# Neighbourhood attention: values and weights each split into two fp32r halves, products of 128 stationary columns, in place of fp32 products

## Chip, cores and metric

The kernel runs on one core of one Trainium2 chip. The metric is device time in microseconds (us) of one execution; lower is better.

## What is computed

One layer of an encoder trunk, on two requests with the same weights: a prompt of 512 tokens ("sequence 0") and a sample of 1024 tokens ("sequence 1"). In the layer a projection feeds two attention branches, a global one (GQA) and a neighbourhood one; their outputs are merged by gates, and a dense MLP follows. The change touches the neighbourhood branch only. Cut to that branch (8 heads of 64 channels, tokens on a grid 64 wide, each token attending to a window of 8 rows by 16 columns):

```python
s = jnp.einsum('bqhd,bqwhd->bhqw', qi, kg).astype(jnp.float32) * scale + bi[None]
p = jax.nn.softmax(s, axis=-1).astype(v.dtype)
return jnp.einsum('bhqw,bqwhd->bqhd', p, vg)
```

All inputs and outputs are fp32.

## The kernel before

The kernel is written with a framework that lists instructions in program order, orders them on each engine by priority and readiness, and places the waits. Nearly all DMAs are issued from one queue, that of SyncE (SP). Nearly every product of the kernel is done in fp32r, a one-pass fp32 format of the TensorE, with each operand split into a high half (a ScalarE copy rounds it to fp32r) and a low half (VectorE subtracts the high half from the original): `wunit` (L93, L94) does that for weights, `mm3` (L112 to L114) multiplies high by high, high by low and low by high.

`run` weaves generators: while an attention (`gqa`, then `na`) of one sequence runs, the projections or gates of another are woven in between, so that TensorE has other work ("fill"). In `attention(0)`, the attention of the prompt, the fill is the projection `proj` of the two halves of the sample (its last step writes the values `vb` to DRAM, L483 to L490). In `attention(1)` the fill is `gates` of the sample and then `out_merge` of the prompt.

`na` works through items (head h, row tile rt, column block b): 8 heads times 4 items in sequence 0, with 256 keys each (`ng` = 2 groups of 128), and 8 heads times 8 items in sequence 1, with 384 keys each (`ng` = 3). For an item:

- `softmax` (L651): two score matmuls S (L658, fp32r, queries stationary); VectorE adds the bias and takes the maximum (L661, L662); ScalarE takes the exponential (L665); VectorE inverts the sum and scales (L666, L667).
- `values` (L670): `ng` transposes on TensorE into the PSUM tile T (L674), then one ScalarE copy T to `pt` (L676).
- `weigh` (L679): `ng` products in plain fp32 (L681), with 64 columns of V stationary and 128 columns of `pt` moving, accumulated into the PSUM tile A. It is issued one item later than `values`.
- `finish` (L684), after four items: VectorE copies A to `o` (L686), and SP stores `o`.

Between heads, `load(h)` brings V, Q and K. V is loaded for two heads at once (16 DMAs, L620, only when h is even), in front of Q (L623) and four K loads (L108) on the SP queue; it has two buffers, one for each pair of heads. `load(h+1)` and the bias table of head h+2 (L636) are issued with the first item of head h.

Of the kernel before, what the change touches and what calls it, by code (L numbers as in the profile page):

```python
# [10 lines left out]
F32 = mybir.dt.float32  # L11
F32R = mybir.dt.float32r
BF16 = mybir.dt.bfloat16
AF = mybir.ActivationFunctionType
ALU = mybir.AluOpType
AX = mybir.AxisListType

P = 128
D = 1024
KT = D // P  # L20
CH = 512
TT = CH // P
GW = 64
HD = 64
# [3 lines left out]
KC0 = (0, 8, 24, 32)  # L28
# [11 lines left out]
class Kern:  # L40
# [371 lines left out]
    def proj(self, ch, U, pool):  # L412
        nc, a = self.nc, self.a
        seq, t0 = ch
        sl = slice(t0, t0 + CH)
        s = self.scr[seq]
        ws = self.stream([a["wq"][i] for i in range(4)] + [a["wkv"][i] for i in range(2)]
                         + [a["wst"][i] for i in range(8)] + [a["wvb"][i] for i in range(4)])
        tq, tk = self.rope_tables(pool, t0)
        done = 0  # L420
        ps = []
        for _ in self.tokmajor(U, ws, 2, 512, ps):
            done += 1
            yield done / 18.0
        rq = []
        for t in range(TT):
            r = pool.tile([P, 512], F32, tag="rq", name="rq", bufs=4)
            nc.scalar.activation(r, ps[t], AF.Copy)
            rq.append(r)
        rk = []  # L430
        norm = self.rope_norm(pool, rq, rk)
        next(norm)
        ps = []
        for _ in self.tokmajor(U, ws, 4, 256, ps):
            done += 1
            yield done / 18.0
        for t in range(TT):
            r = pool.tile([P, P], F32, tag="rk", name="rk", bufs=4)
            nc.scalar.activation(r, ps[t][:, 0:128], AF.Copy)
            rk.append(r)  # L440
            vh = pool.tile([P, 2, 2, HD], F32R, tag="vhl", name="vhl", bufs=2)
            pv = ps[t][:, 128:256].rearrange("p (k d) -> p k d", d=HD)
            nc.scalar.activation(vh[:, :, 0, :], pv, AF.Copy)
            nc.vector.tensor_tensor(vh[:, :, 1, :], pv, vh[:, :, 0, :], op=ALU.subtract)
            r = t0 + t * P
            nc.sync.dma_start(s["va"][r:r + P, :], vh.bitcast(F32).rearrange("p a b d -> p (a b d)"))
        next(norm)
        q2, k2 = [], []

        def q_rope(t):  # L450
            q2.append(self.rope(pool, rq[t], 8, rs[0][:, t * 8:t * 8 + 8], tq[:, 0, t], tq[:, 1, t]))

        def k_rope(t):
            k2.append(self.rope(pool, rk[t], 2, rs[1][:, t * 2:t * 2 + 2], tk[:, 0, t], tk[:, 1, t]))

        def q_stack(hp):
            self.pair_stack(pool, q2, hp, [s["qa"][2 * hp + j][:, sl] for j in range(2)])

        def k_stack(_):
            self.pair_stack(pool, k2, 0, [s["ka"][j][:, sl] for j in range(2)])  # L460

        todo = {2: [(q_rope, 0)], 3: [(q_rope, 1), (k_rope, 0)], 4: [(q_rope, 2), (k_rope, 1)],
                5: [(q_rope, 3), (k_rope, 2)], 6: [(k_rope, 3)],
                7: [(q_stack, 0)], 8: [(q_stack, 1)], 9: [(q_stack, 2)], 10: [(q_stack, 3)], 11: [(k_stack, 0)]}
        for i in range(8):
            ps = self.wstat(next(ws), [U])[0]
            if i < 4:
                self.stack(pool, ps, [s["qb"][2 * i + j][:, sl] for j in range(2)], perm=True)
            else:
                self.stack(pool, ps, [s["kb"][2 * (i - 4) + j][:, sl] for j in range(2)], scale=0.125)  # L470
            if i == 2:
                rs = next(norm)
            for f, x in todo.get(i, ()):
                f(x)
            done += 1
            yield done / 18.0
        ps = []
        for j, _ in enumerate(self.tokmajor(U, ws, 2, 512, ps)):
            for f, x in todo.get(8 + j, ()):
                f(x)  # L480
            done += 1
            yield done / 18.0
        for t in range(TT):  # L483
            v = pool.tile([P, CH], F32, tag="vb", name="vb", bufs=2)
            nc.scalar.activation(v, ps[t], AF.Copy)
            r = t0 // GW + 2 * t
            for hp in range(4):
                for i in range(2):
                    c0 = (r % 4 + i) * GW
                    nc.sync.dma_start(s["vb"][hp][c0:c0 + GW, r // 4], v[i * GW:(i + 1) * GW, hp * P:(hp + 1) * P])  # L490

    def gates(self, chs, Us, pool, func):
        nc, a = self.nc, self.a
# [104 lines left out]
    def na(self, seq, pool, psp):  # L598
        nc, a = self.nc, self.a
# [10 lines left out]
        def load(h):  # L610
            if h in heads:
                return heads[h]
            if h % 2 == 0:
                V = pool.tile([P, 4, rows // 4, P], F32, tag="V", name="V", bufs=2)
                src = s["vb"][h // 2]
                for i in range(4):
                    vr = V[i * 32:(i + 1) * 32]
                    for b in range(4):
                        c0 = i * GW + KC0[b]
                        nc.sync.dma_start(vr[:, b], src[c0:c0 + 32])  # L620
                vals[h // 2] = V
            Q = pool.tile([P, T], F32R, tag="Q", name="Q", bufs=2)
            nc.sync.dma_start(Q.bitcast(F32), s["qb"][h])  # L623
            K = []
# [43 lines left out]
            return p  # L668

        def values(h, rt, b, p, acc):  # L670
            V = vals[h // 2]
            tp = psp.tile([P, NK], F32, tag="T", name="T", bufs=2 if nrt > 1 else 1)
            for g in range(ng):
                nc.tensor.transpose(tp[:, g * P:(g + 1) * P], p[:, g * P:(g + 1) * P], self.ident)  # L674
            pt = pool.tile([P, NK], F32, tag="pt", name="pt", bufs=2)
            nc.scalar.activation(pt, tp, AF.Copy)  # L676
            return lambda: weigh(h, rt, b, V, pt, acc)

        def weigh(h, rt, b, V, pt, acc):  # L679
            for g in range(ng):  # L680
                nc.tensor.matmul(acc[0:64, b * P:(b + 1) * P], V[:, b, rt + g, (h % 2) * 64:(h % 2) * 64 + 64],  # L681
                                 pt[:, g * P:(g + 1) * P], start=g == 0, stop=g == ng - 1)

        def finish(h, rt, acc):  # L684
            o = pool.tile([64, CH], F32, tag="o", name="o", bufs=2)
            nc.vector.tensor_copy(o.rearrange("p (r b c) -> p b r c", b=4, c=16),  # L686
                                  acc[0:64].rearrange("p (b r c) -> p b r c", b=4, c=16))
            nc.sync.dma_start(s["ob"][h * 64:(h + 1) * 64, rt * CH:(rt + 1) * CH], o)

        items = [(h, rt, b) for h in range(8) for rt in range(nrt) for b in range(4)]  # L690
# [235 lines left out]
    def scratch(self):  # L926
        self.scr = []
        for q in range(2):
# [2 lines left out]
            self.scr.append(dict(  # L931
                qa=[t(f"qa{h}_", [P, T]) for h in range(8)], ka=[t(f"ka{h}_", [P, T]) for h in range(2)],
                va=t("va_", [T, 2 * P]), qb=[t(f"qb{h}_", [P, T]) for h in range(8)],
                kb=[t(f"kb{h}_", [P, T]) for h in range(8)], vb=[t(f"vb{h}_", [256, T // 256, P]) for h in range(4)],
                g=[t(f"g{i}_", [P, T]) for i in range(16)], oa=t("oa_", [512, T]), ob=t("ob_", [512, T]),
                x1=t("x1_", [T, D]), u2=[t(f"u2{i}_", [P, T]) for i in range(KT)]))

# [251 lines left out]
```

## Time and profile before

| | |
|---|---|
| median of 3 runs | 2530.9 us (2529.63 to 2534.13) |
| profiled execution, its own time | 2528.55 us |
| its span in the trace | 2526.8 us |
| mean granted TensorE clock | 0.975 of full speed |
| TensorE busy | 2388.2 us (95%) |
| TensorE weight loads | 1898.6 us (75%) |
| VectorE busy | 1472.3 us (58%) |
| ScalarE busy | 971.3 us (38%) |
| GpSimd busy | 330.1 us (13%) |
| DMA, mean | 129 GB/s |

Busy time of TensorE is the sum of matmuls whose ends are modelled; neighbouring matmuls overlap, so their spacing (the difference of two starts) is what one costs, and it is shorter than the duration of one. PE is TensorE's matmul side, PEld its weight loads (the stationary operand), DVE is VectorE, ACT ScalarE, POOL GpSimd, SPq the SyncE queue that issues DMAs. The neighbourhood items of sequence 0 lie at about 490 to 637 us of the span, those of sequence 1 at about 950 to 1157 us.

### The profile page before, as it was taken

The page shows a single profiled execution, that of the slowest core. Times are in us where ns is not written, and L with a number is a line of the kernel's source. Part 1 is how long each engine was busy: PE and PEld are TensorE (multiplying, and loading weights), DVE is VectorE, ACT ScalarE, POOL GpSimd, SP SyncE. Part 2 cuts the span into 40 slices and gives each one's busy share as a digit, 9 for nine tenths or more (in the row PEclk, how much of TensorE's full clock was granted, in tenths as well). Part 3 has the DMA queues.
Part 4 walks back from the last instruction along what each step waited for, and adds up shares of the span by engine and source line. Part 5 has one row for each costly group of instructions (what it writes and reads, how often), then busy time and mean ns, then how long its engine had stood idle before and what let it go on. Part 6 is the DMA issues. An engine that isn't in the chain of part 4 may idle for free.

```text
span 2526.8 us, 29800 instructions
## 1 busy us (share of the span) xinstructions
PE 2388.2 (95%) x10992; PEld 1898.6 (75%) x10992; DVE 1472.3 (58%) x2511; ACT 971.3 (38%) x1589; POOL 330.1 (13%) x278
## 2 busy tenths in 40 slices
PE   5987899979999999989998999999999999999997
PEld 4876777756777777767776788887788888888876
DVE  7987677565477763575867754445733333333466
ACT  4434456434577763554334223222412211221222
POOL 4210021230000003331202000003100000000133
PEclk9998899989999999999999999999999999999999
DMA  6757744565512117585656525334511210211231
GB/s 248 245 185 238 213 119 145 141 187 174 157 55 66 58 50 184 148 235 189 202 188 206 191 69 159 99 90 126 176 40 45 61 48 26 67 50 34 68 116 59
DMA packets 134851, 325.86 MB, mean 129 GB/s; under 512 B 21392, under 2 KB 34224, under 8 KB 134704
## 3 DMA queue, kind: packets, MB, share of 16 engines
q1 hardware_dynamic: 134128, 322.86, 41.8%
q0 software_dynamic: 288, 1.05, 0.3%
q8 instruction: 87, 1.43, 0.2%
q14 instruction: 60, 0.49, 0.1%
q10 hardware_dynamic: 288, 0.03, 0.0%
HBM read 261.99 MB, written 62.93 MB: 129 GB/s over the span
## 4 chain that ended last, share of the span: by engine, by line
PE 68%; DVE 12%; DMA 8%; issue 4%; ACT 3%; POOL 2%; SPq 1%; POOLq 0%; ACTq 0%; DVEq 0%
PE D L112 18%; PE D L114 18%; PE D L113 18%; PE S L535 3%; PE T L553 3%; DVE wlo L94 2%; PE A L681 2%; PE A L566 2%; PE A L567 1%; DMA wraw<-in_wada 1%; PE T L674 1%; DVE junk L248 1%; DMA wraw<-in_wst 1%; ACT whi L93 1%; PE S L658 1%
## 5 line engine op out<-in xcount | busy, mean ns | idle before, releaser
L93 ACT ACTIVATE whi<-wraw 128x1024 fp32r<-128x1024 f32 x266 | 279.4, 1057 | 828.2 <-PE D L114 396.9
L114 PE MATMUL D<-uh,wlo 128*128 128x512 f32 x1344 | 537.2, 400 | 20.5 <-DVE wlo L94 20.5
L112 PE MATMUL D<-uh,whi 128*128 128x512 f32 x1344 | 538.3, 400 | 14.1 <-ACT whi L93 12.5
L113 PE MATMUL D<-ul,whi 128*128 128x512 f32 x1344 | 533.9, 397 | 0.0
L94 DVE TENSOR_TENSOR wlo<-wraw,whi 128x1024 fp32r<-128x1024 f32 x266 | 334.8, 1261 | 336.5 <-ACT whi L93 325.8
L114 PEld LDWEIGHTS D<-uh,wlo 128*128 128x128 f32 x1344 | 256.5, 191 | 78.9 <-DVE wlo L94 23.0
L112 PE MATMUL D<-whi,hh 128*128 128x512 f32 x768 | 304.8, 398 | 6.3 <-ACT hh L864 6.3
L112 PEld LDWEIGHTS D<-uh,whi 128*128 128x128 f32 x1344 | 257.3, 191 | 70.1 <-ACT whi L93 13.8
L114 PE MATMUL D<-whi,hl 128*128 128x512 f32 x768 | 303.7, 397 | 0.8 <-DVE hl L865 0.6
L113 PE MATMUL D<-wlo,hh 128*128 128x512 f32 x768 | 303.4, 397 | 0.0
L113 PEld LDWEIGHTS D<-ul,whi 128*128 128x128 f32 x1344 | 257.0, 191 | 54.7 <-issue 0.5
L886 DVE TENSOR_TENSOR y<-y,D 128x512 f32<-128x512 f32 x168 | 115.1, 685 | 214.8 <-PE D L114 214.2
L112 PEld LDWEIGHTS D<-whi,hh 128*128 128x128 f32 x768 | 145.4, 189 | 43.8 <-ACT hh L864 10.2
L114 PEld LDWEIGHTS D<-whi,hl 128*128 128x128 f32 x768 | 145.3, 190 | 37.3 <-DVE hl L865 3.7
L113 PEld LDWEIGHTS D<-wlo,hh 128*128 128x128 f32 x768 | 145.5, 189 | 33.6
L847 POOL TENSOR_TENSOR y<-y,g 128x1024 f32<-128x1024 f32 x12 | 28.8, 2402 | 867.4 <-DVE y L886 867.4
L538 DVE TENSOR_REDUCE m<-S 128x1 f32<-128x1024 f32 (+1 forms) x96 | 99.7, 1041 | 51.7 <-PE S L535 51.2
L557 DVE TENSOR_TENSOR pl<-T,ph 128x512 fp32r<-128x512 f32 x160 | 107.4, 684 | 16.4 <-ACT ph L556 15.0
L556 ACT ACTIVATE ph<-T 128x512 fp32r<-128x512 f32 x160 | 93.4, 597 | 55.5 <-PE T L553 53.1
L112 PE MATMUL D<-whi,uh 128*128 128x512 f32 (+1 forms) x288 | 105.5, 371 | 2.8 <-ACT whi L93 2.2
L647 POOL TENSOR_TENSOR wm<-Wb,mask 128x384 f32<-128x384 f32 (+1 forms) x96 | 78.4, 830 | 198.4 <-DVE m L661 118.8
L113 PE MATMUL D<-wlo,uh 128*128 128x512 f32 (+1 forms) x288 | 103.6, 360 | 0.0
(159 smaller groups left out, 3700.1 us busy)
## 6 DMA issues: line engine op xcount, KB each, us to landing
wraw<-in_w SPq DMA_DIRECT2D x132, 512.0 KB, 3.7
wraw<-in_wst SPq DMA_DIRECT2D x56, 512.0 KB, 5.4
wraw<-in_wada SPq DMA_DIRECT2D x32, 512.0 KB, 4.3
g<-gst SPq DMA_DIRECT2D x48, 256.0 KB, 2.3
og<-g SPq DMA_DIRECT2D x48, 256.0 KB, 3.2
wraw<-in_wab SPq DMA_DIRECT2D x24, 512.0 KB, 5.2
wraw<-in_wo SPq DMA_DIRECT2D x24, 512.0 KB, 5.1
raw<-in_wada_k SPq DMA_DIRECT2D x16, 512.0 KB, 8.2
```

The source lines that it names most:

```text
L93: nc.scalar.activation(hi, raw, AF.Copy)
L94: (engine or nc.vector).tensor_tensor(lo, raw, hi, op=ALU.subtract)
L112: mm(out, l[0], r[0], start=start, stop=False)
L113: mm(out, l[0], r[1], start=False, stop=False)
L114: mm(out, l[1], r[0], start=False, stop=stop)
L535: nc.tensor.matmul(S[:, k * CH:(k + 1) * CH], q, K[r][:, k * CH:(k + 1) * CH], start=r == 0, stop=r == 1)
L538: nc.vector.tensor_reduce(m, S[:, :T], axis=AX.X, op=ALU.max, negate=True)
L553: nc.tensor.transpose(tp[:, qt * P:(qt + 1) * P], Ps[qt][:, k * P:(k + 1) * P], self.ident)
L556: nc.scalar.activation(ph, tp, AF.Copy)
L557: nc.vector.tensor_tensor(pl, tp, ph, op=ALU.subtract)
L647: nc.gpsimd.tensor_tensor(wm.rearrange("p (r c) -> p r c", c=32), wv, mask[:, rt * 4 + b, :].rearrange("p (r c) -> p r c", c=32), op=ALU.add)
L886: nc.vector.tensor_tensor(y[:, hs], y[:, hs], ps, op=ALU.add)
```

## The change

The values are written to DRAM with the high and the low fp32r half of each head side by side (64 columns each), four heads to a scratch tensor. V is loaded for each head instead of for each pair of heads; a head's V now holds 128 columns (high, low), so a V tile is as large as before. The transposed weights are split too: ScalarE writes the high half `ph`, VectorE the low half `pl`. `weigh` runs 2 times `ng` fp32r products with 128 stationary columns (high and low of V) in place of `ng` fp32 products with 64. The upper 64 partitions of A then hold the low half's part, and `finish` adds them (one ScalarE copy more).

```diff
         for t in range(TT):
-            v = pool.tile([P, CH], F32, tag="vb", name="vb", bufs=2)
-            nc.scalar.activation(v, ps[t], AF.Copy)
             r = t0 // GW + 2 * t
-            for hp in range(4):
+            for hf in range(2):
+                v = pool.tile([P, 4, 2, HD], F32R, tag="vb", name="vb", bufs=2)
+                pv = ps[t][:, hf * 256:(hf + 1) * 256].rearrange("p (h d) -> p h d", d=HD)
+                nc.scalar.activation(v[:, :, 0, :], pv, AF.Copy)
+                nc.vector.tensor_tensor(v[:, :, 1, :], pv, v[:, :, 0, :], op=ALU.subtract)
+                vf = v.bitcast(F32).rearrange("p a b d -> p (a b d)")
                 for i in range(2):
                     c0 = (r % 4 + i) * GW
-                    nc.sync.dma_start(s["vb"][hp][c0:c0 + GW, r // 4], v[i * GW:(i + 1) * GW, hp * P:(hp + 1) * P])
+                    nc.sync.dma_start(s["vb"][hf][c0:c0 + GW, r // 4], vf[i * GW:(i + 1) * GW])
...
-            if h % 2 == 0:
-                V = pool.tile([P, 4, rows // 4, P], F32, tag="V", name="V", bufs=2)
-                src = s["vb"][h // 2]
-                for i in range(4):
-                    vr = V[i * 32:(i + 1) * 32]
-                    for b in range(4):
-                        c0 = i * GW + KC0[b]
-                        nc.sync.dma_start(vr[:, b], src[c0:c0 + 32])
-                vals[h // 2] = V
+            V = pool.tile([P, 4, rows // 4, P], F32R, tag="V", name="V", bufs=2)
+            src = s["vb"][h // 4][:, :, h % 4 * P:(h % 4 + 1) * P]
+            for i in range(4):
+                vr = V[i * 32:(i + 1) * 32].bitcast(F32)
+                for b in range(4):
+                    c0 = i * GW + KC0[b]
+                    nc.sync.dma_start(vr[:, b], src[c0:c0 + 32])
+            vals[h] = V
...
-            pt = pool.tile([P, NK], F32, tag="pt", name="pt", bufs=2)
-            nc.scalar.activation(pt, tp, AF.Copy)
-            return lambda: weigh(h, rt, b, V, pt, acc)
-
-        def weigh(h, rt, b, V, pt, acc):
-            for g in range(ng):
-                nc.tensor.matmul(acc[0:64, b * P:(b + 1) * P], V[:, b, rt + g, (h % 2) * 64:(h % 2) * 64 + 64],
-                                 pt[:, g * P:(g + 1) * P], start=g == 0, stop=g == ng - 1)
+            ph = pool.tile([P, NK], F32R, tag="pt", name="ph", bufs=2)
+            pl = pool.tile([P, NK], F32R, tag="pl", name="pl", bufs=2)
+            nc.scalar.activation(ph, tp, AF.Copy)
+            nc.vector.tensor_tensor(pl, tp, ph, op=ALU.subtract)
+            return lambda: weigh(b, rt, V, (ph, pl), acc)
+
+        def weigh(b, rt, V, pt, acc):
+            for j in range(2):
+                for g in range(ng):
+                    nc.tensor.matmul(acc[:, b * P:(b + 1) * P], V[:, b, rt + g, :], pt[j][:, g * P:(g + 1) * P],
+                                     start=j == 0 and g == 0, stop=j == 1 and g == ng - 1)
 
         def finish(h, rt, acc):
-            o = pool.tile([64, CH], F32, tag="o", name="o", bufs=2)
-            nc.vector.tensor_copy(o.rearrange("p (r b c) -> p b r c", b=4, c=16),
-                                  acc[0:64].rearrange("p (b r c) -> p b r c", b=4, c=16))
+            lo = pool.tile([64, CH], F32, tag="ot", name="ot", bufs=1)
+            nc.scalar.activation(lo, acc[64:128], AF.Copy)
+            o = pool.tile([64, CH], F32, tag="o", name="o", bufs=2 if nrt > 1 else 1)
+            nc.vector.tensor_tensor(o.rearrange("p (r b c) -> p b r c", b=4, c=16),
+                                    acc[0:64].rearrange("p (b r c) -> p b r c", b=4, c=16),
+                                    lo.rearrange("p (b r c) -> p b r c", b=4, c=16), op=ALU.add)
...
-                kb=[t(f"kb{h}_", [P, T]) for h in range(8)], vb=[t(f"vb{h}_", [256, T // 256, P]) for h in range(4)],
+                kb=[t(f"kb{h}_", [P, T]) for h in range(8)], vb=[t(f"vb{h}_", [256, T // 256, CH]) for h in range(2)],
```

## Rows read from the trace of the kernel before

**Rows 1.** Stretches: length; busy PE, PEld, DVE, ACT, POOL; granted clock, DMA share, GB/s.
```profile
490.00:628.00 138.00, 115.50 (x530) 83.95 (x528) 81.68 (x238) 55.96 (x137) 32.82 (x44) 0.89 0.61 179
950.00:1157.00 207.00, 196.83 (x1058) 147.84 (x1057) 116.10 (x373) 94.87 (x226) 68.80 (x70) 0.98 0.67 178
```

**Rows 2.** Timeline of PE, a burst of items in sequence 1: start, us, group.
```profile
1057.73 0.62 PE L658 MATMUL S<-K,Q 128*128 128x384 f32 x2
1058.27 0.87 PE L681 MATMUL A<-pt,V 128*64 128x128 f32 x6
1059.07 0.55 PE L674 MATMUL T<-ident,P 128*128 128x128 f32 x3
1059.38 0.96 PE L658 MATMUL S<-K,Q 128*128 128x384 f32 x4
1060.18 0.49 PE L674 MATMUL T<-ident,P 128*128 128x128 f32 x3
1060.60 0.87 PE L681 MATMUL A<-pt,V 128*64 128x128 f32 x6
```

**Rows 3.** Timeline of PE, one item in sequence 0.
```profile
525.95 0.65 PE L681 MATMUL A<-pt,V 128*64 128x128 f32 x4
526.53 0.50 PE L112 MATMUL D<-uh,whi 128*128 128x512 f32 x1
```

**Rows 4.** Timeline of PE, then of PEld: fp32r, 128 stationary columns, 256 moving.
```profile
318.30 0.28 PE L114 MATMUL D<-whi,ul 128*128 128x256 f32 x1
318.42 0.28 PE L112 MATMUL D<-whi,uh 128*128 128x256 f32 x1
...
318.30 0.19 PEld L112 LDWEIGHTS D<-whi,uh 128*128 128x128 f32 x1
```

**Rows 5.** The bounds: PE, 512 moving columns; PEld, loads before transposes.
```profile
1049.75 0.39 PE L112 MATMUL D<-uh,whi 128*128 128x512 f32 x1
1049.98 0.40 PE L113 MATMUL D<-ul,whi 128*128 128x512 f32 x1
...
1059.07 0.31 PEld L674 LDWEIGHTS T<-ident,P 128*128 128x128 f32 x3 [0.17 <-issue]
```

**Rows 6.** Groups by line and shape: busy, mean ns, idle before it.
```profile
L681 PE MATMUL A<-pt,V 128*64 128x128 f32 x512 | 81.6, 293 | 5.0 <-ACT pt L676 4.8
L674 PEld LDWEIGHTS T<-ident,P 128*128 128x128 f32 x256 | 30.1, 146 | 27.7 <-issue 12.1 <-ACT pt L676 4.5 <-PE T L674 2.0
L557 DVE TENSOR_TENSOR pl<-T,ph 128x512 fp32r<-128x512 f32 x160 | 107.4, 684 | 16.4 <-ACT ph L556 15.0
L661 DVE CUSTOM_DVE_ANT_0 sb<-S,wm 128x384 f32<-128x384 f32 x64 | 34.9, 550 | 53.6 <-PE S L658 51.7 <-PE T L674 1.3 <-POOL wm L647 0.3
L667 DVE TENSOR_SCALAR P<-P,z 128x384 f32<-128x384 f32 x64 | 31.0, 485 | 1.2
L575 DVE TENSOR_TENSOR o<-A,ot 64x512 f32<-64x512 f32 x24 | 16.3, 681 | 3.2 <-ACT ot L573 2.7
L686 DVE COPY o<-A 64x512 f32<-64x512 f32 x24 | 16.3, 678 | 5.8 <-PE A L681 5.7
L573 ACT ACTIVATE ot<-A 64x512 f32<-64x512 f32 x24 | 14.3, 596 | 9.1 <-PE A L567 8.8
```

**Rows 7.** Timeline of the SP queue: V and K loads, and value stores.
```profile
493.51 14.39 SPq L620 DMA_DIRECT2D V<-vb  x16
508.41 2.38 SPq L108 DMA_DIRECT2D K<-kb  x4
628.23 8.99 SPq L490 DMA_DIRECT2D vb<-vb  x14
1064.08 8.64 SPq L620 DMA_DIRECT2D V<-vb  x16
```

**Rows 8.** Who waited for whom, 485 to 640 us: total, times, longest.
```profile
PE S L658 <- DMA K<-kb: 4.5, 4, 2.3
```

**Rows 9.** Busy time in a stretch behind a V load.
```profile
1070.00:1100.00 30.00, 24.19 (x135) 17.34 (x135) 22.23 (x77) 18.14 (x47) 12.32 (x13) 0.89 0.81 213
```

More of the change, by code (lines that the diff above doesn't have):

```diff
@@ L670, in values @@
         def values(h, rt, b, p, acc):
-            V = vals[h // 2]
+            V = vals[h]
             tp = psp.tile([P, NK], F32, tag="T", name="T", bufs=2 if nrt > 1 else 1)
```

## The prediction

> **What bounds the kernel now.** I read the page of the profile first (TensorE 95% busy), then the busy time of the engines in stretches, to see whether that share holds where the change lies. In the stage of sequence 1 it does, with 197 of 207 us; in that of sequence 0 TensorE is busy for 115.5 of 138 us, at a mean granted clock of 0.89, so there it spends part of the time at the lower of its levels, 1.2 GHz in place of 2.4, after idle stretches [rows 1]. VectorE, to which the change gives work, is busy for 82 of 138 and 116 of 207 us [rows 1]. So in sequence 1 whatever TensorE saves should show in the end, as long as nothing else becomes late; in sequence 0 only part of it can.
>
> Then I read the timeline of PE by starts, since a duration overstates what a matmul costs. In a burst of items the reader is to see three things [rows 2]: six fp32 instructions (L681) take 0.80 us from their first start to the next group's start; three transposes take 0.31 us when scores follow, but 0.42 when fp32 products follow; and two scores take 0.54 us before fp32 products where four take 0.80. Fp32 products thus come some 0.11 to 0.14 us late, whatever stands in front of them. Last I read the SP queue and the waits, because the change doubles the V loads.
>
> **The products.** An fp32 product leaves two records on PE: 512 of them [rows 6] for 8 heads times (4 items times 2 groups + 8 items times 3 groups) = 256 products. The changed kernel has as many: 2 halves times 256 = 512. Only the price of one changes. Before, the groups cost 64 x 0.80 [rows 2] + 32 x 0.58 [rows 3] = 69.8 us, and the late starts 96 x 0.14 = 13.4 us.
>
> No fp32r matmul with 128 moving columns is in the trace. The nearest row has 128 stationary and 256 moving columns: starts 0.12 us apart, and the stationary load of one starts 0.12 us before its matmul, with the matmul in front [rows 4]. That the load sets this pace as much as the columns do is how I read it: then half the columns still cost 0.12, since the next stationary matrix needs as long as before. From below, loads for the transposes follow each other in (0.31 - 0.14) / 2 = 0.085 us (three in 0.31, one lasting about 0.146 [rows 6]) [rows 5]. From above, if few moving columns gain nothing, or the format needs several passes on a short operand, the 0.23 us of 512 columns [rows 5]. I take 0.12, the row that is nearest in shape. The groups then cost 64 x 0.72 + 32 x 0.48 = 61.4 us, 8.4 us less. The late start should go too, since the stationary load of an fp32r matmul runs under the matmul in front of it [rows 4]: 13.4 us less. Sum on TensorE: -21.8 us, of which sequence 1 has 64 x 0.22 = 14.1 and sequence 0 the other 7.7. The bounds: at 0.085 the groups cost 43.5 us, in all -39.7; at 0.23 they cost 117.8 us, in all +34.6.
>
> On this price the Trainium skill has two rules that differ. TensorE: Matmul & The Clock Gate, LDWEIGHTS, has a load take its columns divided by 1.2, an estimate of 107 ns for 128 columns; the spacing of 0.12 us here agrees roughly, and the groups would cost 54.6 us. The same page, Back-to-back issue gap, gives about 81 ns for a stream with 128 moving columns, by which they would cost 41.5 us; no row here shows an fp32r pair that fast.
>
> **VectorE and ScalarE.** The low half `pl` is new: 96 subtractions. The same form costs 0.684 us at 512 columns [rows 6]; for 384 columns I take the 0.55 us of L661, which reads as many from PSUM [rows 6], and for 256, on the same line, 0.42, so 64 x 0.55 + 32 x 0.42 = 48.6 us. 24 subtractions of the value stores add 24 x 0.42 = 10 us; `finish` swaps a copy of 0.678 for an add of 0.681, and adds 24 ScalarE copies of 0.596 us, 14.3 in all [rows 6]. I cost all of that at nothing: in sequence 1 VectorE goes from 116 to 151 of 207 us, and woven-in matmuls cover it. `pl` is used one item later, so it is not on an item's own chain; but T comes free only after it, and it stands in VectorE's queue in front of the next item's maximum. If the fill is gone, an item of sequence 1 has about 1.4 us of VectorE work (0.55 and 0.485 [rows 6], the rest small instructions, an estimate) and would have 1.95, against 1.66 on TensorE now (two scores 0.40, three transposes 0.32, products 0.94) and 1.44 after. There the pace would be +0.3 us an item, not -0.22.
>
> **The SP queue.** V is loaded 8 times a sequence in place of 4. One load takes 8.64 us of the SP queue in sequence 1, and up to 14.39 us in sequence 0 [rows 7]: 4 x 8.6 = 34 and up to 4 x 14.4 = 58 us more. Value stores fall from 96 to 48, at 8.99 / 14 = 0.64 us [rows 7] some 31 us less, spread over three projections, under matmuls; I count that as nothing. Also, V of head h+1 now needs the buffer of head h-1, and so waits for that head's last products, which come an item or two into head h; before, the buffer was long free. Behind it in program order stand Q and K of head h+1, and then stores and weight loads of the fill.
>
> What a V load in front costs can be read twice. In sequence 0, the 14.39 us in front of Q and K [rows 7] go with the 4.5 us for which scores wait for K in that stage [rows 8]: one of three loads that fall between heads, 1.5 us a load. In sequence 1, the load at 1064 us [rows 7] is followed by a stretch in which TensorE is busy for 24.2 of 30 us [rows 9]: at most 5.8 us, again for one of three, 1.9 us a load. With 7 between heads in place of 3, at the same rate: 4 x 1.5 + 4 x 1.9 = +13.6 us. From below this is 0, if the framework puts Q and K in front of a V load that is not ready; from above every one of the 7 costs the full price, 7 x 4.5 - 4.5 = +27 and 7 x 5.8 - 5.8 = +35 us.
>
> **Sum.** -21.8 + 13.6 = -8.2 us against the profiled execution's 2528.55 us (1.7 above its span): 2520.3. That execution is 2.4 us under the median shown, and the forecast is meant for the median: 2530.9 - 8.2 = 2523.
>
> **Rivals.**
> 1. Slower: few moving columns are dear in fp32r. For it: fp32 itself needs two instructions to a product, and no row shows this format under 256 columns. Against: at 256, the pace is already as low as the stationary load explains. Where TensorE sets the end, every 0.01 us on a product is 5.1 us; the forecast turns into a loss from (83.2 - 13.6) / 512 = 0.136 us a product. At 0.23: +34.6 + 13.6 = +48, about 2579; at 0.20, +19 + 13.6 = +33, about 2564.
> 2. Slower: K waits behind V in sequence 0. A head lasts 138 / 8 = 17 us there [rows 1]; V (up to 14.4) and K (2.4) [rows 7] nearly fill it, and V starts late. All 7 loads at 4.5 us: -21.8 + 27 + 7.6 = +13, about 2544. It decides once about 22 us of such waits are added, as TensorE's gain is then gone.
> 3. No change: VectorE takes the gain in bursts. If 42% of the items run without fill, +0.3 us there and -0.22 elsewhere cancel; with the 13.6 us of waits 15% are enough (96 x (0.22 - 0.52 x 0.15) = 13.6). About 2531. For it speaks that items do come in bursts [rows 2]; against it, that woven work lies between bursts.
> 4. Faster by more: the loads follow each other at 0.085 us. -39.7 + 13.6 = -26, about 2505. Its page is that of the back-to-back gap above.
>
> **Chances and range.** The forecast, faster by 5 to 15 us: 0.36 (2516 to 2526). Rival 1: 0.14; rival 2: 0.20; rival 3: 0.24; rival 4: 0.06. A measurement of this kernel tells about 0.2% (5 us) from no change. Faster 0.42 (forecast and rival 4), same 0.24, slower 0.34. The range goes from 2508 (rival 4's edge) to 2562: what is left out is most of rival 1 and the far end of rival 4.
>
> **What would show it.** Right: in the changed trace, groups of six fp32r products span 0.70 to 0.75 us to the next group's start, and transposes in front of them keep 0.31; PE busy in the stage of sequence 1 falls with its length. Wrong: a spacing of 0.2 us or more (rival 1); waits of scores for K, or SP waiting at V for TensorE, of over 20 us in the stage of sequence 0 (rival 2); the end of the stages unmoved with VectorE over 80% busy in them and transposes waiting for `pl` (rival 3). Wrong from another side it would be if the order of the woven work came out so differently that the end of the attention stages moved by more than these terms.

## The result, and the profile after

| | before | after |
|---|---|---|
| median | 2530.57 us (2529.63 to 2534.13) | 2600.53 us (2595.11 to 2601.64) |
| span of the profiled execution | 2526.8 us | 2599.9 us |
| mean granted TensorE clock | 0.975 | 0.953 |

The changed kernel takes 1.0265 times as long, interval 1.0244 to 1.0286: 70 us slower where the forecast was 8 us faster, and outside the range.

Where the time went is seen first in the busy time of the engines in three stretches (columns as in [rows 1]). In the kernel before:

```profile
480.00:720.00 240.00, 216.79 (x1009) 163.46 (x1009) 136.72 (x316) 111.78 (x224) 37.01 (x49) 0.93 0.55 158
720.00:960.00 240.00, 239.89 (x1211) 187.14 (x1211) 165.61 (x245) 164.87 (x262) 3.97 (x5) 1.00 0.22 60
960.00:1240.00 280.00, 268.89 (x1364) 205.02 (x1362) 171.96 (x450) 121.76 (x260) 79.39 (x73) 0.99 0.67 191
```

The same stretches in the kernel after:

```profile
480.00:720.00 240.00, 188.14 (x783) 144.46 (x782) 125.43 (x316) 91.45 (x195) 33.09 (x44) 0.79 0.55 158
720.00:960.00 240.00, 239.49 (x1224) 187.42 (x1223) 178.14 (x265) 176.00 (x279) 0.58 (x1) 1.00 0.18 55
960.00:1240.00 280.00, 250.35 (x1225) 207.27 (x1224) 163.40 (x459) 117.31 (x262) 72.27 (x73) 0.87 0.61 169
```

The middle stretch, global attention without neighbourhood items, is as it was. In the two others TensorE stands idle for 81.5 us (520 - 188.1 - 250.4) in place of 34.3, and what it does, it does at a mean clock of 0.79 and 0.87 in place of 0.93 and 0.99.

These stretches have fixed ends while the stages move, so the second view takes the items of each sequence from their first score to their last product. In the kernel before (not quite where they were placed ahead of the prediction: those of sequence 0 end at 628 us, and those of sequence 1 start at 968, 18 us behind the start of the 207 us of [rows 1]):

```profile
490.80:627.70 136.90, 114.59 (x525) 83.20 (x523) 81.27 (x236) 55.12 (x135) 32.82 (x44) 0.89 0.61 179
968.30:1154.50 186.20, 176.03 (x969) 130.96 (x967) 113.73 (x370) 92.09 (x222) 64.81 (x66) 0.98 0.67 180
```

In the kernel after:

```profile
482.60:657.20 174.60, 129.76 (x524) 100.21 (x524) 91.54 (x269) 56.38 (x142) 33.09 (x44) 0.73 0.52 150
1003.30:1225.30 222.00, 192.35 (x971) 161.16 (x970) 146.09 (x435) 102.11 (x238) 64.57 (x66) 0.84 0.61 172
```

With practically as many matmuls as before the items take 175 us in place of 137 and 222 in place of 186. These 38 and 36 us, less the 8 us by which the items of sequence 0 start earlier, are 66 of the 73 us between the two spans.

The products answer to [rows 2]. First a pair in sequence 0, then a burst in sequence 1 (timeline of PE after: start, us, group, idle before):

```profile
529.53 0.42 PE L686 MATMUL A<-ph,V 128*128 128x128 f32 x2
529.78 0.39 PE L686 MATMUL A<-pl,V 128*128 128x128 f32 x2
...
1153.37 0.84 PE L686 MATMUL A<-ph,V 128*128 128x128 f32 x3
1154.01 0.84 PE L686 MATMUL A<-pl,V 128*128 128x128 f32 x3
1154.65 1.59 PE L660 MATMUL S<-K,Q 128*128 128x384 f32 x4
```

Two products take 0.25 us at 529 us, where the clock is full: 0.125 each, as forecast. Six take 1.28 us at 1153 us, 0.213 each: the clock granted from 1151 to 1156 us is 0.50, the lower level.

The SP queue answers to [rows 7]. V loads follow one after another, each 10 to 14 us long, with Q and K of their head behind them (timeline of the SP queue after):

```profile
482.03 11.27 SPq L622 DMA_DIRECT2D V<-vb  x16
...
497.22 12.92 SPq L622 DMA_DIRECT2D V<-vb  x16
510.18 0.58 SPq L625 DMA_DIRECT2D Q<-qb  x1
510.81 2.40 SPq L108 DMA_DIRECT2D K<-kb  x4
```

And the waits of PE from 480 to 1240 us (total, times, longest), against the 4.5 us of [rows 8]; the low half `pl` appears as a cause:

```profile
PE S L660 <- DMA K<-kb: 14.1, 6, 5.9
PE A L686 <- DVE pl L680: 13.6, 12, 4.6
...
PE T L676 <- DVE pl L680: 4.6, 4, 2.2
```

The longest wait for K stands behind the V load at 493 us before, and behind the one at 497 us after (timeline of PE, before, then after). Behind the later V loads of sequence 0 in the kernel before, at 541 and 574 us ([rows 7] have the one at 493), no score waits for K:

```profile
512.38 0.48 PE L658 MATMUL S<-K,Q 128*128 128x256 f32 x2 [2.30 <-DMA K<-kb]
...
514.94 1.45 PE L660 MATMUL S<-K,Q 128*128 128x256 f32 x4 [5.89 <-DMA K<-kb]
```

The new subtractions cost in duration what [rows 6] led to expect (groups by line and shape: 0.554 us at 384 columns against 0.55, 0.418 at 256 against 0.42; those of the value stores took 24 x 0.422 = 10.1 us, against 10):

```profile
L680 DVE TENSOR_TENSOR pl<-T,ph 128x384 fp32r<-128x384 f32 x64 | 35.2, 554 | 19.3 <-ACT ph L679 19.1
L680 DVE TENSOR_TENSOR pl<-T,ph 128x256 fp32r<-128x256 f32 x32 | 13.4, 418 | 16.9 <-ACT ph L679 16.4
```

The longest wait for `pl`, though, does not come from the length of a subtraction (timeline of VectorE, then of PE):

```profile
540.51 1.77 DVE L373 TENSOR_TENSOR rq<-rq,rsr 128x512 f32<-128x512 f32 x1
...
546.22 0.41 DVE L680 TENSOR_TENSOR pl<-T,ph 128x256 fp32r<-128x256 f32 x1
...
546.69 0.69 PE L686 MATMUL A<-pl,V 128*128 128x128 f32 x2 [4.55 <-DVE pl L680]
```

From 540.5 to 546.2 us VectorE works on the rotary embedding of the woven-in projection (L373, L381); the low half stands behind it, and its product waits 4.55 us. Before the wait of 2.78 us at 1209 us it is an instruction of the woven-in `out_merge` (L768), which itself had waited 1.82 us for ScalarE.

### The profile page after: what moved, and what is told of

It is laid out like the page before. It is cut to its first block, busy times and chain, and to the rows that moved or that the text cites. A ratio compares the mean times of both kernels' runs of the same rounds, so it can differ in the third digit from the quotient of the medians.

```text
span 2599.9 us, 30013 instructions
## 1 busy us (share of the span) xinstructions
PE 2418.0 (93%) x10992; PEld 1943.8 (75%) x10992; DVE 1526.8 (59%) x2631; ACT 988.9 (38%) x1625; POOL 330.8 (13%) x278
## 4 chain that ended last, share of the span: by engine, by line
PE 64%; DVE 13%; DMA 9%; issue 4%; ACT 3%; SPq 3%; POOL 2%; POOLq 0%; DVEq 0%; ACTq 0%
PE D L112 17%; PE D L114 17%; PE D L113 17%; PE S L538 3%; PE T L556 3%; DMA wraw<-in_wst 2%; DVE wlo L94 2%; PE A L569 1%; SPq L622 1%; DMA wraw<-in_wada 1%; PE A L570 1%; PE A L686 1%; DVE junk L248 1%; ACT whi L93 1%; DMA Wb<-in_rpb 1%
## 5 line engine op out<-in xcount | busy, mean ns | idle before, releaser
L93 ACT ACTIVATE whi<-wraw 128x1024 fp32r<-128x1024 f32 x266 | 279.4, 1057 | 855.2 <-PE D L114 404.3
L560 DVE TENSOR_TENSOR pl<-T,ph 128x512 fp32r<-128x512 f32 x160 | 107.0, 684 | 14.1 <-ACT ph L559 13.0
```

Of the source, the lines that this page charges most:

```text
L93: nc.scalar.activation(hi, raw, AF.Copy)
L560: nc.vector.tensor_tensor(pl, tp, ph, op=ALU.subtract)
```

## Experiments

Theories at the start: the added V loads on the SP queue (rival 2's mechanism, at a higher price); the low half on VectorE (rival 3's); the fp32r products (rival 1's); and the order of woven work. Every ratio is to the kernel before, run on the same chip (medians 2527.7 to 2529.8 us).

### One part of the change at a time

**V for each head**, nothing else: the fp32 V of the pair is loaded again for the second head.

```diff
-            if h % 2 == 0:
-                V = pool.tile([P, 4, rows // 4, P], F32, tag="V", name="V", bufs=2)
...
-                vals[h // 2] = V
+            V = pool.tile([P, 4, rows // 4, P], F32, tag="V", name="V", bufs=2)
...
+            vals[h] = V
```

> One part alone: the kernel before, but V loaded for every head (16 DMAs each, 8 loads a sequence in place of 4), everything else as before. Theory Q (the SP queue): the 128 added V loads hold the SP queue for some 8 to 14 us a load, Q and K of the next head and the fill's weights come late, and this alone gives most of the loss: 35 to 75 us over the kernel before, with scores waiting for K some 10 us more in the stage of sequence 0. Theory D (VectorE's low half, which holds T and stands in an item's way): 0 to 10 us. Theory C (the short fp32r products, and the clock that falls with them): 0 to 10 us.

Measured: 2595.75 us, ratio 1.0262 (1.0245 to 1.0279), +67 us. This part alone is worth nearly the whole loss. From 480 to 720 us TensorE is busy for 180 us, less than after (columns as above):

```profile
480.00:720.00 240.00, 180.10 (x767) 131.94 (x767) 106.66 (x270) 79.97 (x176) 36.81 (x49) 0.80 0.53 153
```

What is late shows in the SP queue of this kernel, from 574 us on:

```profile
574.16 13.02 SPq L619 DMA_DIRECT2D V<-vb  x15
...
593.42 0.43 SPq L622 DMA_DIRECT2D Q<-qb  x1
593.89 2.37 SPq L108 DMA_DIRECT2D K<-kb  x4
596.37 0.64 SPq L635 DMA_DIRECT2D Wb<-in_rpb  x1
597.05 0.49 SPq L687 DMA_DIRECT2D ob<-o  x1
597.59 0.58 SPq L88 DMA_DIRECT2D wraw<-in_wvb  x1
```

Behind V stand Q and K, the bias table, and then `wraw`, a weight block of the fill's projection. By the chain of waits its transfer ends at 604.7, ScalarE splits it (L93), and the fill starts at 605.86, after idle time put down to `whi` (timeline of PE):

```profile
605.86 1.65 PE L112 MATMUL D<-whi,uh 128*128 128x512 f32 x3 [0.71 <-ACT whi L93]
```

Over 480 to 1240 us the fill's wait is the largest of PE; in the trace before, the same wait is 1.6 us, and scores wait 8.8 us for `m`:

```profile
PE D L112 <- ACT whi L93: 23.6, 5, 19.0
PE S L657 <- DVE m L660: 23.2, 21, 8.8
PE S L657 <- DMA K<-kb: 10.7, 8, 4.4
```

Of the 23.6 us, 19.0 are one wait at the end of sequence 0 (SP queue, then PE). There the next weights stand behind 25 value stores of the fill; in the trace before 14 are left at that point, and no such wait follows:

```profile
654.85 16.68 SPq L490 DMA_DIRECT2D vb<-vb  x25
...
672.85 1.07 SPq L88 DMA_DIRECT2D wraw<-in_wst  x2
...
677.77 0.80 PE L112 MATMUL D<-uh,whi 128*128 128x512 f32 x1 [18.96 <-ACT whi L93]
```

The changed kernel has half as many of these stores, and its only wait for `whi` in the same stretch is 4.4 us. So up to some 15 of the 67 us (an estimate, 19.0 - 4.4) may belong to the stores of before and not to the change.

So a late V load holds up the item and the work that was to fill its gaps. While the fill waits, items stand alone and run at the pace of their own chain.

**The low half**, computed and not used.

```diff
             nc.scalar.activation(pt, tp, AF.Copy)
+            pl = pool.tile([P, NK], F32R, tag="pl", name="pl", bufs=2)
+            nc.vector.tensor_tensor(pl, tp, pt, op=ALU.subtract)
```

> One part alone: the kernel before plus the subtraction of the low half (T minus its copy), whose result nothing reads. Theory D: T comes free later and VectorE has 48 us more, 15 to 50 us over the kernel before. Theories Q and C: 0 to 10 us.

Measured: 2540.54 us, 1.0041 (1.0025 to 1.0057), +12 us, between what the theories gave (10 at most, 15 at least). The prediction put it at nothing.

**The products**: two passes of the unsplit `pt` in fp32r over 128 columns of V, without the low halves.

```diff
-            for g in range(ng):
-                nc.tensor.matmul(acc[0:64, b * P:(b + 1) * P], V[:, b, rt + g, (h % 2) * 64:(h % 2) * 64 + 64],
+            for j in range(2):
+                for g in range(ng):
+                    nc.tensor.matmul(acc[:, b * P:(b + 1) * P], V[:, b, rt + g, :], pt[:, g * P:(g + 1) * P],
```

> One part alone: the kernel before with fp32r products of 128 stationary columns, two passes that both move the ScalarE copy; there is no low half, V holds two heads' unsplit values in its 128 columns, so the attention output is another one. Theory C: the short products let the granted clock fall in the bursts, 15 to 50 us over the kernel before. Theories Q and D: the products alone are cheaper, at 0.12 us each at the full clock, 5 to 22 us under the kernel before.

Measured: 2556.46 us, 1.0104 (1.008 to 1.0127), +28 us, where the sum of the prediction has -21.8. Yet the price of a product is the predicted one at full clock (timeline of PE of this kernel):

```profile
1057.34 0.49 PE L674 MATMUL T<-ident,P 128*128 128x128 f32 x3
1057.58 0.87 PE L682 MATMUL A<-pt,V 128*128 128x128 f32 x6
1058.28 0.74 PE L658 MATMUL S<-K,Q 128*128 128x384 f32 x3
```

Six take 0.70 us, and transposes in front of them 0.24, less than the 0.31 expected: the late start is gone. The loss lies elsewhere, and the runs on the products below look for it.

**The stores**: values written by 2 DMAs a tile in place of 8 (the changed kernel writes 4).

```diff
-            for hp in range(4):
-                for i in range(2):
-                    c0 = (r % 4 + i) * GW
-                    nc.sync.dma_start(s["vb"][hp][c0:c0 + GW, r // 4], v[i * GW:(i + 1) * GW, hp * P:(hp + 1) * P])
+            for i in range(2):
+                c0 = (r % 4 + i) * GW
+                nc.sync.dma_start(s["vb"][c0:c0 + GW, r // 4], v[i * GW:(i + 1) * GW])
```

> One part alone: the kernel before with values stored by 2 DMAs a tile in place of 8, into one scratch tensor of 512 columns (unsplit fp32), V loaded in the same number of DMAs but in runs of 512 bytes. In the changed trace the attention of the prompt starts 7 us earlier than before. If the stores are why: 3 to 9 us under the kernel before. If the SP queue is bound by the bytes or the runs of a V load and not by the number of DMAs: slower than before by 5 us or more, with V loads of over 9 us of the queue in sequence 1.

Measured: 2517.99 us, 0.9958 (0.9943 to 0.9972), -11 us. Fewer stores win time, and the prediction counted them at nothing. It is not the change's own number: this kernel has 24 stores, the changed one 48, the one before 96. And the gain is net of dearer V loads: from the one scratch tensor of 512 columns a V DMA takes 0.594 us of the queue at the median, as in the changed kernel (0.593), against 0.419 before. In the changed kernel the scores of sequence 0 start at 482.6 us, against 490.8 before.

The four parts sum to 67 + 12 + 28 - 11 = +96 us, against +70: they are not additive, and the first and the last differ from the change in their stores.

### What of a V load costs

**Half as many DMAs**: `before_v8` is before with the stores grouped and two column blocks in each V DMA, so 8 in place of 16 a load.

```diff
-                    for b in range(4):
-                        c0 = i * GW + KC0[b]
-                        nc.sync.dma_start(vr[:, b], src[c0:c0 + 32])
+                    for b in (0, 2):
+                        sv = src[i * GW + KC0[b]:i * GW + KC0[b] + 32]
+                        nc.sync.dma_start(vr[:, b:b + 2], bass.AP(tensor=sv.tensor, offset=sv.offset, ap=[
+                            list(sv.ap[0]), [8 * sv.ap[0][0], 2]] + [list(x) for x in sv.ap[1:]]))
```

> The kernel before with the values kept by pair of heads in one scratch tensor, stored by 2 DMAs a tile in place of 8, and V loaded by 8 DMAs in place of 16, each over two column blocks in runs of 2 KB (1 KB in sequence 0). Theory Q: the number of DMAs on the SP queue is what costs, so a V load takes some 4 us of it in place of 8, and the time falls below that of the grouped stores alone: 12 to 30 us under the kernel before. If instead the loads were hidden: as grouped stores alone, 8 to 12 us under.

Measured: 2502.87 us (2499.8 to 2504.64), 0.9899 (0.9882 to 0.9915). It is the fastest kernel of the study: 27 us under the one before, and 16 under `stores_alone`. The 16 go with half as many V DMAs and with a shorter queue time of each, 0.425 us in place of 0.594, as the scratch is again one for each pair of heads.

**V for each head on top of it**, then with three buffers:

```diff
-            if h % 2 == 0:
...
-            V = pool.tile([P, 4, rows // 4, P], F32, tag="V", name="V", bufs=2)
+            V = pool.tile([P, 4, rows // 4, P], F32, tag="V", name="V", bufs=3)
```

> The kernel before with the cheaper V loads (8 DMAs, 2502.9 so far), but V loaded for every head: as many V DMAs in all as the kernel before had. Theory N (the number of DMAs on the SP queue is what costs): near the kernel before with grouped stores, 2505 to 2525. Theory W (each load now waits for the buffer of the head before last, and what stands behind it waits too): 2530 to 2560, whatever the DMAs cost.

> The same with three buffers for V in place of two, so that the load of the next head waits for no product of the head before. Theory W: falls by 10 us or more against two buffers. Theory N: within 6 us of two buffers.

Measured: 2540.73 us, 1.0051 (1.0035 to 1.0068), 38 us above `before_v8`; with three buffers 2537.09 us, 1.0041 (1.0025 to 1.0058). The wait for a free buffer, which the prediction named, is worth 4 us at most here, less than the two intervals leave open.

**V from another queue**: as `v_per_head`, issued by GpSimd.

```diff
-                    nc.sync.dma_start(vr[:, b], src[c0:c0 + 32])
+                    nc.gpsimd.dma_start(vr[:, b], src[c0:c0 + 32])
```

> As V for every head in 16 DMAs (2595.8), but the V loads are issued from GpSimd's queue in place of SP's. Theory Q (what costs is SP's time and what stands behind the loads on SP): most of the 67 us go, 2500 to 2545, unless GpSimd's own work, the bias sums, comes late instead. If the transfers themselves cost (DMA engines, HBM): still above 2575.

Measured: 2551.68 us, 1.0092 (1.0064 to 1.012). The same bytes and buffers, and 43 of the 67 us are gone (24 are left, a little more than expected): they belonged to SP's queue. The fill's wait for `whi` falls from 23.6 to 1.4 us. The other 24 are not told apart; one new wait is that GpSimd's bias sums come late, since its own instructions now stand behind DMA issues (waits of 480 to 700 us):

```profile
DVE sb L660 <- POOL wm L646: 18.4, 5, 12.0
```

The Trainium skill says in DMA: Bandwidth & Descriptors, Rules for kernel authors, that DMAs spread over several engines gain no bandwidth and only save issue time. This run agrees on what is saved, at 43 us, and does not test the bandwidth.

The queue time of a V DMA (least, median and most, in ns, behind the count) in the kernel before:

```profile
L620 SPq DMA_DIRECT2D V<-vb x128: 302/419/1552, 474.4 to 1072.3; - x128
```

In `v_per_head`, twice as many at the same median:

```profile
L619 SPq DMA_DIRECT2D V<-vb x256: 302/419/2160, 475.4 to 1166.4; - x128
```

And in the kernel after, of whose 256 DMAs 249 lie between 470 and 1240 us:

```profile
L622 SPq DMA_DIRECT2D V<-vb x249: 538/593/1560, 472.5 to 1167.5; - x125
```

Counts times medians give an estimate of the time that V takes of SP: 54 us before, 107 in `v_per_head`, 152 after, 76 in `stores_alone`, 27 in `before_v8`, and 54 in `v_per_head_v8` and `after_v8`. The price of a microsecond of queue is no constant. Loads added between heads cost 1.2 to 1.4 us for each: 54 more cost 67 us in `v_per_head` (the late stores above among them), 27 more cost 38 in `v_per_head_v8`. Where the loads stay in their places and only their time changes, it is 0.3: 49 fewer from `stores_alone` to `before_v8` save 16 us, 97 more from `after_v8` to after cost 29. So loads that stand between heads where none stood cost more than shorter loads give back.

### Why the products made it slower

Counts of bursts come from the starts on PE in sequence 1: a burst is a run of S, T and A without a projection or gate matmul D in between; the last one, which no D ends, is left out.

**One pass and four** in place of two (`range(2)` in `weigh`, 256 and 1024 products):

> As the fp32r products alone, but one pass in place of two: 256 products in place of 512, some 31 us less work on TensorE at the full clock; the output is half. Theory C (the bursts are paced by VectorE and ScalarE, so less product work only makes idle time in which the clock falls): no faster than the products alone, 2550 to 2575, with at least as much time at the lower clock. Theory P (the products' price itself is what made them slower): 2520 to 2535.

> As the fp32r products alone, but four passes in place of two: 1024 products in place of 512, some 61 us more work on TensorE at the full clock; the output is double. Theory C: part of the added work falls into idle time and the clock holds up better, so less than 25 us over the products alone, with less time at the lower clock. Theory P: 50 to 80 us over the products alone.

Measured: 2513.17 us, 0.9938 (0.9923 to 0.9953), and 2655.2 us, 1.0497 (1.0482 to 1.0513). One pass gains 17 us over fp32, the second costs 43 and the next two 99, so 0.17 to 0.19 us a product, more than the 0.12 of the full clock. Both lie outside what was expected. The bursts change with it: 35 before, of which 5 last over 4 us and take 78 us; 35 (5, 72 us) with one pass; 22 (10, 117 us) with two; 13 (7, 191 us) with four. (V for each head does it too: 26, of which 7 take 104 us. The changed kernel has 28, of which 10 take 132.) With four passes, TensorE works in such a burst without a pause at the lower clock. Two groups of the timeline of PE in this kernel:

```profile
1071.14 2.80 PE L682 MATMUL A<-pt,V 128*128 128x128 f32 x12
1073.74 0.95 PE L658 MATMUL S<-K,Q 128*128 128x384 f32 x2
```

And the busy time of a stretch around them:

```profile
1059.00:1090.00 31.00, 31.00 (x139) 30.18 (x138) 11.79 (x42) 8.67 (x24) 6.86 (x8) 0.50 0.32 86
```

Twelve products take 2.60 us, 0.217 each, at clock 0.50 with 31 of 31 us busy.

**Price or order?** `products_64` keeps two passes with 64 stationary columns; `products_half_columns` keeps those and their number, but each product moves 64 columns in place of 128.

```diff
-                    nc.tensor.matmul(acc[:, b * P:(b + 1) * P], V[:, b, rt + g, :], pt[:, g * P:(g + 1) * P],
+                    nc.tensor.matmul(acc[0:64, b * P:(b + 1) * P], V[:, b, rt + g, (h % 2) * 64:(h % 2) * 64 + 64], pt[:, g * P:(g + 1) * P],
...
+                    c = b * P + j * 64
+                    nc.tensor.matmul(acc[0:64, c:c + 64], V[:, b, rt + g, (h % 2) * 64:(h % 2) * 64 + 64],
+                                     pt[:, g * P + j * 64:g * P + j * 64 + 64], start=g == 0, stop=g == ng - 1)
```

> As the fp32r products alone, two passes, but with 64 stationary columns, those of the head itself (the output is double): 512 products as before. If the load of 128 stationary columns sets the pace: a product takes 0.06 to 0.08 us at the full clock where it took 0.12, and the time falls from 2556 to 2510 to 2535. If the format itself sets it, by its 128 moving columns: within 8 us of 2556, at 0.12 us a product.

> As the fp32r products with 64 stationary columns, 512 of them, but the two passes are replaced by two halves: each product moves 64 of the 128 columns into its own half of the result (so the sum is that of one pass in fp32r, with the low halves left out). The number of matmuls is that of the two passes, the moving columns are those of one. Theory O (the order that the framework plans, which takes two passes for dearer than they are): items in some 35 bursts as before, 2505 to 2525. Theory I (the price of the instructions, or the clock under short matmuls): as with two passes of 64 stationary columns, 2540 to 2556, as the stationary loads are the same.

Measured: 2547.84 us, 1.0072 (1.0049 to 1.0096), and 2522.65 us, 0.9983 (0.997 to 0.9997). With 64 stationary columns a product costs half as much (timeline of PE of `products_64`, at clock 1.00):

```profile
1017.80 0.58 PE L682 MATMUL A<-pt,V 128*64 128x128 f32 x6
1018.21 0.57 PE L658 MATMUL S<-K,Q 128*128 128x384 f32 x2
```

Six take 0.41 us, 0.068 each; other groups of six at the full clock give 0.06 to 0.075. Yet this half price brings back only some 9 us of the 28, and the intervals of the two kernels overlap; 21 or more were expected. `products_64` has the same order of instructions as `products_alone` on VectorE, ScalarE, GpSimd and SP, and as few bursts (22; 10, 113 us). `products_half_columns` has as many products and stationary loads as `products_64`, but 33 bursts (6, 81 us), and is 23 us faster against its own before. Its price is nearly the same, 0.37 us for six (timeline of PE, clock 1.00):

```profile
1060.91 0.54 PE L683 MATMUL A<-pt,V 128*64 128x64 f32 x6
1061.28 0.42 PE L658 MATMUL S<-K,Q 128*128 128x384 f32 x1
```

In the whole trace its products are busy for 56 us and those of `products_64` for 65, so at most 9 of the 23 us can be their price. The busy times of 960 to 1180 us in `products_64`:

```profile
960.00:1180.00 220.00, 175.88 (x1035) 143.52 (x1034) 123.69 (x375) 94.12 (x224) 67.25 (x67) 0.90 0.61 166
```

The same stretch in `products_half_columns`:

```profile
960.00:1180.00 220.00, 196.35 (x1146) 156.00 (x1145) 131.21 (x390) 106.19 (x242) 70.39 (x68) 0.95 0.71 196
```

TensorE idles 44 us with the one and 24 with the other. (The second stretch holds some 30 us behind its last item; cut to the items, 968 to 1175 and 969 to 1150 us, it is 44 of 207 and 24 of 181 us.) So most of the loss goes with the order in which the woven work comes out, long bursts without fill, and not with the price of a product. No run sets the order by itself, so that it is the cause is argued from these kernels and not shown. That order follows the number of moving columns and passes and not the stationary columns; that the framework reckons such products dearer than they are is my reading, since no trace shows its reckoning.

### The changed kernel with cheap loads

`after_v8` is the changed kernel with 8 V DMAs a head and the scratch laid out by head (as `before_v8`); `after_v8_no_low` also leaves out the subtraction and moves the high half twice.

```diff
-            nc.vector.tensor_tensor(pl, tp, ph, op=ALU.subtract)
-            return lambda: weigh(b, rt, V, (ph, pl), acc)
+            return lambda: weigh(b, rt, V, (ph, ph), acc)
```

> The changed kernel with V loaded by 8 DMAs in place of 16 for each head, in longer runs from a scratch tensor that is laid out by head: as many V DMAs in all as the kernel before has. Theory Q: most of the loss goes, 2530 to 2560, that is within 30 us of the kernel before. What is then left over the kernel before with the same cheaper loads is theories C and D together: 20 to 50 us. If the waits for V's two buffers, and not the queue's time, are the cause: still above 2580.

> The changed kernel with the cheaper V loads and without the low half of the weights: the second pass moves the high half again, and VectorE's subtraction of the weights is gone (that part of the values' product is left out and another doubled). Against the same kernel with the low half (2571.5): if the low half costs here what it costs alone, 12 us, 2553 to 2565; if its cost is hidden behind the products' and the loads', above 2566. Against V for every head with the same loads: the products cost their 28 us again, or more.

Measured: 2571.46 us, 1.017 (1.0154 to 1.0185), and 2551.42 us, 1.0096 (1.0067 to 1.0125). Both miss what was expected: with cheap loads 42 us are left over the kernel before, not 30 at most; the low half is worth 20 us and not 12, the products less than 28. A chain from the fastest kernel to the changed one follows, in which each step adds what its row names:

| step | us | adds |
|---|---|---|
| `before_v8` | 2502.9 | |
| V for each head (`v_per_head_v8`) | 2540.7 | +37.8 |
| split values, 48 stores for 24, two-pass fp32r products (`after_v8_no_low`) | 2551.4 | +10.7 |
| low half of the weights (`after_v8`) | 2571.5 | +20.0 |
| 16 V DMAs a head, scratch of four heads (after) | 2600.5 | +29.1 |

37.8 + 29.1 = 67 of the 98 us lie in how V is laid out and loaded. In `after_v8` scores wait for K no more, and the products wait 16.4 us for `pl` (10 times, longest 7.8).

## Why the prediction was wrong

**The step that failed is the SP queue**, the term of +13.6 us. Its mechanism was right, and its price was off: alone this part measured +67, with cheap loads +38, and even the upper bounds, +27 and +35, sum to less than the 67. The price came from what waits for K and idle time behind a load cost before, 1.5 and 1.9 us a load [rows 7 to 9]. That measures a queue which had slack: of the three V loads between heads of sequence 0 only the first made scores wait for K, by 3.1 of the 4.5 us. Two V loads now stand where one stood, and what is late next is not only K but the fill's weight blocks further back in the queue (PE waits for `whi` 23.6 us in `v_per_head`, 1.6 before; 4.4 in the changed kernel, where the stores are fewer and scores wait 14.1 us for K). The prediction named those stores and weight loads as standing behind, and gave them no price. Also a V DMA of the changed kernel takes 0.593 us of the queue, not 0.419.

**Stores at nothing**: -11 us in `stores_alone`, which goes further than the change; the change's own 48 stores were not tried alone. "Under matmuls" was true of TensorE, but the queue of those stores is what V, Q and K come through.

**The products**: the sizing held at the full clock (0.125 in pairs, 0.70 us for six in `products_alone`), so rival 1's price is wrong. That the saving of 21.8 us reaches the end did not hold: this part alone gave +28, in the chain +10.7. The prediction took the order of work as given and named its change only as what would make it wrong "from another side". The Trainium skill's rule that a stationary load takes its columns divided by 1.2 (TensorE: Matmul & The Clock Gate, LDWEIGHTS) roughly agrees at both sizes run here: an estimate from it is 53 ns for 64 columns and 107 for 128, against measured products of 0.068 and 0.12 us. The 81 ns of the same page's Back-to-back issue gap were not seen at 128 stationary columns.

**VectorE at nothing**: wrong by 12 us alone and 20 in the changed kernel. VectorE is at 146 of the 222 us of the items of sequence 1 (66%), below rival 3's mark of 80%, yet products and transposes wait for `pl` (13.6 and 4.6 us). The prediction had the low half covered by woven-in matmuls; the fill also brings work of its own to VectorE, and in the longest waits `pl` stands behind that.

**The rivals.** Rival 2 named the right mechanism, and 2544 us was 56 too low. Its sign, over 20 us, does not show by its letter: from 470 to 700 us scores wait 14.1 us for K, and SP waits at V for TensorE for 0.7 us; another 14.4 us of SP at V are put down to `Wb`. A product cheaper than rival 4's 0.085 us was seen only with 64 stationary columns.

**Still open**: how much of the 67 us of `v_per_head` the stores of before make; how the 10.7 us of the products in the chain part into order and clock; what the 24 us are that remain when V leaves SP's queue; and the split products under the order of before, which wasn't tried.

## What to carry to other kernels

Where nearly all DMAs leave from one queue, cost a change by the queue time that it adds (count times the time of one in the trace) and ask for all that stands behind it, the loads of woven-in work above all. Here a microsecond of queue cost 1.2 to 1.4 us where loads were added between heads, and 0.3 where they only grew longer; a wait read from a queue with slack prices the next load too low. Fewer, larger DMAs were worth more here (-27 us) than any change to the products. A cover such as "matmuls in between" holds only as long as the order stays, and woven-in work also queues on the engine whose work it is to cover; so look at the bursts without fill, and at what stands ahead on that engine, before counting work at nothing.

## What the runs showed of the hardware

- Short fp32r products (128 moving columns) cost 0.12 us with 128 stationary columns and 0.06 to 0.075 with 64, at full clock; at 1.2 GHz 0.213 to 0.217 with 128. With 64 stationary columns 64 moving ones cost 0.062, hardly less than 128.
- A stretch of 31 us in which TensorE had no idle time ran at 1.2 GHz throughout; it held short products, transposes and scores.
- A V DMA took 0.42 us of SP's queue at the median from a scratch of one pair of heads or one head, whether it brought one column block or two, and 0.59 from a scratch of four or eight heads.
